# Background steps and weight halves ordered behind the sums and results, in the Strassen-like input projection of a one-core fp32 block

## The chip, the cores and the metric

The kernel runs on one core of one Trainium2 chip. The metric is the device time of one execution in microseconds (us). Engines are named as in the profile: PE is TensorE, DVE is VectorE, ACT is ScalarE, POOL is GpSimd, SP is SyncE. ACT, POOL and SP also issue DMAs.

## The reference

One layer of a hybrid encoder, sequence 1024, width 1024, float32:

```python
h = rmsnorm(x, g_pre_mix)
u_pool, q, k, v = split(h @ w_in)            # 512 columns each
y_pool = multiscale_pool(u_pool) @ w_br_pool # 4 groups of 128, windows 2, 4, 8, 16
y_sb   = stick_breaking_attention(q, k, v) @ w_br_sb     # 8 heads of 64
gates  = sigmoid(h @ w_gate + b_gate)        # 2 x 1024 columns
m = (gates[:, :1024] * y_pool + gates[:, 1024:] * y_sb) @ w_out
x = x + rmsnorm(m, g_post_mix)
h2 = rmsnorm(x, g_pre_mlp)
x = x + rmsnorm(relu(h2 @ w_up)**2 @ w_down, g_post_mlp)  # w_up to 4096 columns
```

## The kernel before, in words

Every large product of float32 matrices is made of three products on PE: an operand is cast into a high part on ACT (`hi`), and the rest is its low part, a subtraction on DVE (`lo`). Lines 110, 111 and 112 of the function `mm3` are hi·hi, hi(weight)·lo(data) and lo(weight)·hi(data). A weight tile `whi`/`wlo`, `a0hi`/`a0lo` and so on is thus usable in two steps: after its cast on ACT (line 1191) and after its subtraction on DVE (line 1192).

The kernel runs in stages: input norm, projection, attention with the pooling branch, output product, MLP. The change lies in the projection, `phase_project`. It computes the gates and q and k in twelve **pairs** (`PAIRS`: gates 0 to 4, q0, k0, q1, k1, gates 5 to 7). A pair is a 2x2 block product made with seven products instead of eight, in the Strassen manner. Each of the seven is twelve matmuls (four 128-row blocks times three) of 128x512 into one bank of PSUM, named `sw` in the profile. Their order is b11, b21, t2, t3, t1, t4, b22. The weight operands of a pair come from two loads of 512 KB (`r1`, `r2`, tiles `wraw` and `wrawx`): `a1` (all of r1, for b11 and b21), `a22` (half of r2, for t4), `sb` and `sa`, which are sums of halves and are made in place by four additions on DVE (lines 519 to 523), for t2/b22 and t3/t1. Tiles of `sb` are named `s0` or `s1`, of `a22` `a0` or `a1`, of `a1` and `sa` `w`.

The results of the seven products go through sums on DVE (lines 684 to 705): `c11`, `u`, `v`, `c22`, and from there to `result`: a gate goes through a sigmoid on ACT and a store from ACT's queue; q and k are split in a high part (ACT, line 542) and a low part (DVE, line 543) in a staging tile of `self.mx` (`m0` or `m1` in turns, so two are in flight) and stored by POOL to the scratch tensors `qscr`, from which SP loads the operands `qq` and `kk` of the attention. PSUM banks are taken in turns from three pools of 2, 2 and 3, so a bank is written again some seven products later, once DVE or ACT has read it.

Two kinds of work run beside the products. `sw_weights(i + 1)` is a generator that loads and splits the weights of the next pair; one step is taken after each product. `later` is a background generator, again a step or two after each product: for the four groups of the pooling branch it loads `u` (from `uscr`, ACT's queue), makes the window sums `win` (line 581, tiles `m1` and `m2`), splits them into `ph` and `pq`, multiplies them on PE (`dm`, and one `sw` bank), and stores `win` and `u` to `yscr` from POOL's queue; then for eight blocks it loads two shifted copies of v (`vpair`), subtracts them, splits the difference (`vs`) and stores it to `sscr`.

Which instruction stands where in an engine's queue is not the order of the source: a scheduler orders each engine's instructions by its own model of times, under the data dependencies. `tc.issue_after(ins)` adds an edge to that: what is written in its scope stands behind `ins` in the queue of `ins`'s own engine. It adds no wait between engines. `self.behind(ins)` is the same, or nothing where there is no `ins`. Each engine executes its queue strictly in order, so an instruction that waits holds everything behind it.

Of the kernel before, what the change touches and what calls it, by code (L numbers as in the profile page):

```python
# [32 lines left out]
P = 128  # L33
H = 512
# [18 lines left out]
class Block:  # L53
# [113 lines left out]
    def build(self):  # L167
# [55 lines left out]
        self.op7, self.sw, self.heads = {}, {}, {}  # L223
        self.phase_in()
# [303 lines left out]

    def staged(self, shape, dt, name):
        self.turn += 1  # L530
        return self.mx.tile(shape, dt, name=name, tag=f"m{self.turn % 2}")

    def result(self, kind, f, h, t, sign):

        nc = self.nc
        c = slice(h * H, h * H + H)
        if kind == "g":
            nc.scalar.activation(t, t, AF.Sigmoid, bias=self.vt[:, V_BG + f : V_BG + f + 1], scale=sign)
# [3 lines left out]
        nc.scalar.activation(e[:, 0, :], t, AF.Copy, scale=sc)  # L542
        nc.vector.scalar_tensor_tensor(
            out=e[:, 1, :], in0=t, scalar=sc, in1=e[:, 0, :].bitcast(F32), op0=ALU.mult, op1=ALU.subtract
        )
        for b in range(2):
            scr, s = self.qscr[kind == "k"][2 * f + b], e[64 * b : 64 * b + 64].bitcast(F32)
            nc.gpsimd.dma_start(scr[0:128, c].rearrange("(n p) c -> p n c", n=2), s)
            if kind == "q":
                nc.gpsimd.dma_start(scr[128:192, c], s[:, 0, :])  # L550

    def later(self, newbank):
# [19 lines left out]
        yield  # L572
        for g in range(4):
            iu = 3 * (g % 2)
            u = nxt_u
            cur, n = u, 0
            for i in range(g + 1):
                sh = 1 << i
                n = 1 + i % 2
                nxt = whole(n, name="win")  # L580
                nc.vector.tensor_add(nxt[:, sh:], cur[:, sh:], cur[:, : 1024 - sh])
                nc.vector.tensor_copy(nxt[:, :sh], cur[:, :sh])
                cur = nxt
                yield
# [9 lines left out]
            nc.scalar.copy(ph, cur)  # L594
            nc.vector.tensor_sub(pq, cur, ph.bitcast(F32))
# [17 lines left out]
        for t in range(NK):  # L613
# [9 lines left out]
            e = e.rearrange("p (h x) -> p h x", h=8)  # L623
            v = self.mx.tile([P, 8, P], F32R, name="vs", tag=f"m{n + 1}")
            nc.scalar.copy(v[:, :, 0:64], e)
# [20 lines left out]
    def phase_project(self):  # L646
# [16 lines left out]
        nxt = iter(())  # L663
# [12 lines left out]

        begun = {}

        def begin(i):
# [3 lines left out]
            nc.scalar.copy(u, product(w["a1"], 0, "b11"))  # L683
            nc.vector.tensor_add(c11, u, product(w["a1"], 512, "b21"))
# [3 lines left out]
        for i, (kind, f1) in enumerate(self.PAIRS):  # L688
            f2 = f1 + (8 if kind == "g" else 2)
            w = self.sw[i]  # L690
            nxt = self.sw_weights(i + 1) if i + 1 < len(self.PAIRS) else iter(())
# [3 lines left out]
            nc.vector.tensor_add(u, u, product(w["sb"], 0, "t2"))  # L695
            nc.vector.tensor_add(v, u, product(w["sa"], 0, "t3"))  # L696
            d = product(w["sa"], 512, "t1")
            nc.vector.tensor_add(c22, v, d)
            nc.vector.tensor_add(u, u, d)
# [3 lines left out]
            nc.vector.tensor_add(v, v, product(w["a22"], 0, "t4"))  # L703
            self.result(kind, f2, 0, v, -1.0)
            nc.vector.tensor_add(u, u, product(w["sb"], 512, "b22"))
            self.result(kind, f1, 1, u, 1.0)
        self.run(bg)
# [949 lines left out]
```

## Time and profile before

| | us |
|---|---|
| median of 3 runs | 1271.47 (1271.03 to 1273.86) |
| profiled execution, its own time | 1273.6 |
| its span in the profile | 1271.6 |
| PE busy in the span | 1242.0 (98%) |
| DVE busy | 968.9 (76%) |
| ACT busy | 622.6 (49%) |
| POOL busy | 179.7 (14%) |
| granted PE clock, mean | 0.997 |

The span is cut here at 98.5, 342, 365, 580, 760 and 1245 us. The projection's products lie between 98.76 and 347.4, the attention from there to about 580, the rest is the output product and the MLP. The profile's tables give, for a group of instructions, its busy time, the mean duration, and the idle time of the engine just before it with what ended that; rows of a timeline give the start, the duration and in brackets the idle time before with its releaser. A duration includes some overlap with the next instruction: DVE starts a 128x512 subtraction 0.60 us and a 128x1024 one 1.13 us after the one before, though the rows show 0.68 and 1.22.

### The profile page before, as it was taken

How to read it: one execution, taken by the hardware profiler on the slowest of the kernel's cores; microseconds unless marked ns; L12 is line 12 of the kernel's file. 1: busy time of each engine (PE TensorE's matmuls, PEld its weight loads, DVE VectorE, ACT ScalarE, POOL GpSimd, SP SyncE). 2: the span in 40 equal slices, each digit the busy share in tenths (PEclk: the TensorE clock that was granted, in tenths of full speed). 3: DMA queues.
4: the chain of work that ended last, by engine and by line, in shares of the span. 5: the costliest groups of instructions: out<-in, count | busy, mean ns of one | idle time of the engine just before them, and what ended most of it. 6: DMA issues, size and time to landing. Idle time of an engine off the chain costs nothing.

```text
span 1271.6 us, 16184 instructions
## 1 busy us (share of the span) xinstructions
PE 1242.0 (98%) x5707; PEld 1021.7 (80%) x5707; DVE 968.9 (76%) x1311; ACT 622.6 (49%) x994; POOL 179.7 (14%) x319
## 2 busy tenths in 40 slices
PE   9999999999999999999999999999999999999998
PEld 6887777887877877787778878888888888888887
DVE  8749687867578998877797879887865565776975
ACT  7237334333455565664556546455454443344452
POOL 1212111342101111101100002222121110001000
PEclk9999999999999999999999999999999999999999
DMA  6486878977899664456647677666549996556552
GB/s 218 152 245 161 241 195 232 315 262 251 300 356 332 218 209 103 130 129 220 214 139 259 199 247 257 236 225 226 180 181 336 305 302 227 198 198 248 193 197 67
DMA packets 110305, 283.00 MB, mean 223 GB/s; under 512 B 12464, under 2 KB 17584, under 8 KB 109072
## 3 DMA queue, kind: packets, MB, share of 16 engines
q1 hardware_dynamic: 65696, 165.28, 37.4%
q0 software_dynamic: 30992, 91.13, 25.2%
q10 hardware_dynamic: 13536, 25.57, 6.3%
q8 instruction: 45, 0.74, 0.2%
q14 instruction: 36, 0.29, 0.1%
HBM read 208.52 MB, written 94.37 MB: 238 GB/s over the span
## 4 chain that ended last, share of the span: by engine, by line
PE 73%; DMA 10%; DVE 8%; issue 5%; ACT 2%; POOL 1%; ACTq 0%; SPq 0%; DVEq 0%; POOLq 0%
PE d L110 17%; PE d L111 17%; PE d L112 17%; DMA vpair<-vscr 3%; PE dbr L112 3%; PE dbr L111 3%; PE o L838 3%; PE dbr L108 2%; DMA yscr<-win 2%; PE at L814 2%; DMA qscr<-qs 1%; DVE T L801 1%; PE z L794 1%; PE z L797 1%; DMA vscr<-ev 1%
## 5 line engine op out<-in xcount | busy, mean ns | idle before, releaser
L111 PE MATMUL d<-blo,whi 128*128 128x512 f32 (+1 forms) x456 | 172.3, 378 | 0.0
L112 PE MATMUL d<-bhi,wlo 128*128 128x512 f32 (+1 forms) x456 | 171.9, 378 | 0.0
L110 PE MATMUL d<-bhi,whi 128*128 128x512 f32 (+1 forms) x456 | 168.7, 378 | 0.0
L111 PEld LDWEIGHTS d<-blo,whi 128*128 128x128 f32 x456 | 85.7, 188 | 16.1
L112 PEld LDWEIGHTS d<-bhi,wlo 128*128 128x128 f32 x456 | 85.8, 188 | 16.0
L110 PEld LDWEIGHTS d<-bhi,whi 128*128 128x128 f32 x456 | 85.5, 188 | 15.8
L801 DVE TENSOR_TENSOR_SCAN T<-T,past 128x512 f32<-128x512 f32 (+3 forms) x64 | 84.8, 1345 | 8.5 <-ACT T L799 8.4
L111 PE MATMUL d<-b_lo,whi 128*128 128x512 f32 x196 | 76.2, 390 | 1.0 <-DVE b_lo L1083 1.0
L110 PE MATMUL d<-b_hi,whi 128*128 128x512 f32 x196 | 75.8, 390 | 0.1
L112 PE MATMUL d<-b_hi,wlo 128*128 128x512 f32 x196 | 74.2, 389 | 0.0
L78 DVE TENSOR_TENSOR wlo<-wraw,whi 128x1024 fp32r<-128x1024 f32 x45 | 54.8, 1219 | 16.1 <-ACT whi L76 14.4
L76 ACT CAST whi<-wraw 128x1024 fp32r<-128x1024 f32 x45 | 47.4, 1054 | 40.0 <-PE d L111 20.4
L799 ACT ACTIVATE T<-z 128x256 f32<-128x256 f32 (+2 forms) x96 | 44.5, 494 | 40.1 <-PE z L797 36.2
L1380 DVE TENSOR_TENSOR wlo<-slots_hi,whi 128x1024 fp32r<-128x1024 f32 x29 | 35.5, 1223 | 37.0 <-ACT whi L1378 36.9
L1378 ACT CAST whi<-slots_hi 128x1024 fp32r<-128x1024 f32 x29 | 30.5, 1052 | 67.1 <-PE d L111 60.9
L110 PE MATMUL sw<-h_hi,whi 128*128 128x512 f32 x144 | 56.6, 393 | 2.7 <-DVE v L696 0.8
L1378 ACT CAST whi<-slots_lo 128x1024 fp32r<-128x1024 f32 x27 | 28.4, 1053 | 62.3 <-PE d L111 52.1
L824 ACT CAST ahi<-at 128x512 fp32r<-128x512 f32 (+1 forms) x96 | 43.9, 483 | 28.2 <-PE at L814 23.7
L111 PE MATMUL sw<-h_lo,whi 128*128 128x512 f32 x144 | 56.1, 389 | 0.0
L825 DVE TENSOR_TENSOR alo<-at,ahi 128x512 fp32r<-128x512 f32 (+1 forms) x96 | 49.9, 543 | 7.6 <-ACT ahi L824 7.2
L112 PE MATMUL sw<-h_hi,wlo 128*128 128x512 f32 x144 | 55.5, 390 | 0.1
L1380 DVE TENSOR_TENSOR wlo<-slots_lo,whi 128x1024 fp32r<-128x1024 f32 x27 | 33.0, 1221 | 27.0 <-ACT whi L1378 26.9
(446 smaller groups left out, 3436.3 us busy)
## 6 DMA issues: line engine op xcount, KB each, us to landing
wraw<-w SPq DMA_DIRECT2D x57, 512.0 KB, 4.8
ext_b<-ascr SPq DMA_DIRECT2D x40, 512.0 KB, 7.1
wscr<-w POOLq DMA_DIRECT2D x32, 512.0 KB, 9.2
slots_hi<-w SPq DMA_DIRECT2D x10, 1024.0 KB, 8.1
slots_lo<-w SPq DMA_DIRECT2D x10, 1024.0 KB, 8.5
qq<-qscr SPq DMA_DIRECT2D x32, 256.0 KB, 5.7
pscr<-p SPq DMA_DIRECT2D x32, 256.0 KB, 3.9
u<-pscr ACTq DMA_DIRECT2D x32, 256.0 KB, 4.2
```

The source lines that it names most:

```text
L76: nc.scalar.copy(hi, raw)
L78: self.lows.append(nc.vector.tensor_sub(lo, raw, hi.bitcast(F32)).ins)
L110: nc.tensor.matmul(ps, wh, rh, start=first and i == 0, stop=False)
L111: nc.tensor.matmul(ps, wh, rl, start=False, stop=False)
L112: self.last_mm = nc.tensor.matmul(ps, wl, rh, start=False, stop=last and i == n - 1).ins
L799: self.after = nc.scalar.activation(f, z[:, :n], AF.Sigmoid, scale=-1.0)
L801: nc.vector.tensor_tensor_scan(f[:, ::-1], f[:, ::-1], past[:, ::-1], 1.0, ALU.mult, ALU.max)
L824: self.att_hi = nc.scalar.copy(hi[:, c:], at[:, c:]).ins
L825: self.att_lo = nc.vector.tensor_sub(lo[:, c:], at[:, c:], hi[:, c:].bitcast(F32)).ins
L838: t = nc.tensor.matmul(o[:, c0:], v, part[:, c0:], start=s == 0 and part is hi, stop=last and part is lo)
L1378: last_split[0] = nc.scalar.copy(hi, src).ins
L1380: last_split[1] = nc.vector.tensor_sub(lo, src, hi.bitcast(F32)).ins
```

## The change

It has five parts.

1. **Weights.** `sw_weights` (called once per pair, both loads at once, seven products ahead) is replaced in the loop by `sw_later`, a generator for pair j+2 that is started at product 7j+4 and does one small step per product: load of r1 ten products before the pair's first, load of r2 seven before it, then the casts and subtractions of `a1` and `a22`, the four sums, `sb`, and `sa`, a step each. Low parts come one product later than high parts.
2. **Order.** Each step of `sw_later` and of the background `later`, and each low part of q and k, is written in the scope of `behind(act_main)` and `behind(dve_main)`, where `act_main` and `dve_main` are the last cast or sigmoid of a result and the last sum of a product written so far. So on ACT and on DVE these stand behind them in the queue.
3. **Results of q and k.** A staging tile now holds the high parts of two results, and the low part is written over the result tile itself, one product later. Four results can be in flight where two could. The stores are 64x512 pieces: 80 DMAs from POOL's queue where there were 48, with the same bytes.
4. **Windows.** The tiles of the window sums go on alternating between `m1` and `m2` from one group to the next, where each group began at `m1`, so a group's first window is no longer written into the tile of which the group before is still being stored.
5. **Steps.** The background has some more steps (after the cast of `ph`, and around `vs`), one fewer for the first five blocks of v, and takes its double steps until product 42 where it was 36.

The numbers of instructions on PE, DVE and ACT are the same.

```diff
+    def sw_later(self, i):
...
+        pool = self.sw_pools[i % 2]
+        w = self.sw[i] = {}
+        r1 = load(a)
+        for _ in range(3):
+            yield
+        r2 = load(a + n)
+        a11, a12, a21, a22 = r1[:, :512], r1[:, 512:], r2[:, :512], r2[:, 512:]
+        yield
+        w["a1"] = high(r1, self.wp, "w", 3)
+        yield
+        low(w["a1"], r1)
+        yield
+        w["a22"] = high(a22, pool, f"a{i % 2}", 1, 512)
+        yield
+        low(w["a22"], a22)
+        nc.vector.tensor_add(a22, a21, a22)
+        nc.vector.tensor_add(a21, a11, a21)
+        nc.vector.tensor_add(a11, a11, a22)
+        nc.vector.tensor_add(a12, a12, a11)
+        yield
+        w["sb"] = high(r1, pool, f"s{i % 2}", 1)
+        yield
+        low(w["sb"], r1)
+        w["sa"] = high(r2, self.wp, "w", 3)
+        yield
+        low(w["sa"], r2)
...
-        e = self.staged([P, 2, H], F32R, f"{kind}s")
-        nc.scalar.activation(e[:, 0, :], t, AF.Copy, scale=sc)
-        nc.vector.scalar_tensor_tensor(
-            out=e[:, 1, :], in0=t, scalar=sc, in1=e[:, 0, :].bitcast(F32), op0=ALU.mult, op1=ALU.subtract
-        )
-        for b in range(2):
-            scr, s = self.qscr[kind == "k"][2 * f + b], e[64 * b : 64 * b + 64].bitcast(F32)
-            nc.gpsimd.dma_start(scr[0:128, c].rearrange("(n p) c -> p n c", n=2), s)
-            if kind == "q":
-                nc.gpsimd.dma_start(scr[128:192, c], s[:, 0, :])
+        if not self.stage:
+            e = self.staged([P, 2, H], F32R, f"{kind}s")
+            self.stage = [e[:, 0, :], e[:, 1, :]]
+        hi = self.stage.pop(0)
+        self.act_main = nc.scalar.activation(hi, t, AF.Copy, scale=sc).ins
+
+        def low():
+            nc.vector.scalar_tensor_tensor(
+                out=t.bitcast(F32R), in0=t, scalar=sc, in1=hi.bitcast(F32), op0=ALU.mult, op1=ALU.subtract
+            )
+            parts = (hi.bitcast(F32), t, hi.bitcast(F32)) if kind == "q" else (hi.bitcast(F32), t)
+            for b in range(2):
+                scr = self.qscr[kind == "k"][2 * f + b]
+                for n, e in enumerate(parts):
+                    nc.gpsimd.dma_start(scr[64 * n : 64 * n + 64, c], e[64 * b : 64 * b + 64])
+
+        self.lower.append(low)
...
+        n = 2
         for g in range(4):
             iu = 3 * (g % 2)
-            u = nxt_u
-            cur, n = u, 0
+            cur = u = nxt_u
             for i in range(g + 1):
                 sh = 1 << i
-                n = 1 + i % 2
+                n = 3 - n
...
         def product(w, at, name):
             d = newbank()
             self.half(d, w, at, name)
-            next(nxt, None)
-            next(bg, None)
             c = next(count)
-            if c % 6 == 5 and c < 36:
-                next(bg, None)
+            lower, self.lower = self.lower, []
+            with self.behind(self.act_main), self.behind(self.dve_main):
+                for f in lower:
+                    f()
+                if c % 7 == 4 and c // 7 + 2 < len(self.PAIRS):
+                    gens.append(self.sw_later(c // 7 + 2))
+                for gen in gens:
+                    next(gen, None)
+                for _ in range(2 if c % 6 == 5 and c < 42 else 1):
+                    next(bg, None)
             if c % 3 == 2 and c < 48:
                 self.sum_piece_with(self.last_mm)
             return d
+
+        def add(out, a, b):
+            self.dve_main = nc.vector.tensor_add(out, a, b).ins
```

The sums of the loop are made with `add` and keep their places. In the changed source their line is 750, the four weight sums are lines 570 to 573, the window sum is line 643, weight subtractions are lines 553 and 1268, the low part of q and k is line 603.

What the scheduler makes of it is shown at three places, before and after apart.

**DVE, pair 0 to pair 1.** `s0lo` is the last weight part of pair 0; `wraw_1045` is the second load of pair 1, and its addition with `wrawx` (line 521 before, 571 now) is what `sa` of pair 1, and so its products t3 and t1, wait for. Before, from the row behind `s0lo_995` on:

```order
L581 TENSOR_TENSOR win_1114<-u_1024 128x1023
L582 COPY win_1114<-u_1024 128x1
L684 TENSOR_TENSOR c11_1029<-u_1028,sw_1052 128x512
L1192 TENSOR_TENSOR a1lo_1066<-wraw_1045,a1hi_1065 128x512
L586 SCALAR_TENSOR_TENSOR win_1114<-win_1114,u_1024 128x1022
L589 TENSOR_TENSOR win_1114<-win_1114,rcnt_190 128x2
L519 TENSOR_TENSOR wraw_1045<-wraw_1045 128x512
L1192 TENSOR_TENSOR wlo_1048<-wrawx_1043,whi_1047 128x1024
L695 TENSOR_TENSOR u_1028<-u_1028,sw_1075 128x512
L590 TENSOR_TENSOR win_1114<-win_1114,u_1024 128x2
L521 TENSOR_TENSOR wraw_1045<-wrawx_1043,wraw_1045 128x512
```

The addition is the eleventh row behind `s0lo`, and one sum of a product (c11 of line 684) and one more (u of line 695) stand ahead of it. Now, from the twelfth row behind `s0lo_995` on:

```order
L750 TENSOR_TENSOR u_1030<-u_1030,sw_1109 128x512
L570 TENSOR_TENSOR wraw_1045<-wraw_1045 128x512
L652 TENSOR_TENSOR win_1105<-win_1105,u_1024 128x2
L750 TENSOR_TENSOR v_1067<-v_1067,sw_1136 128x512
L750 TENSOR_TENSOR u_1030<-u_1030,sw_1160 128x512
L571 TENSOR_TENSOR wraw_1045<-wrawx_1028,wraw_1045 128x512
L750 TENSOR_TENSOR c11_1181<-u_1180,sw_1213 128x512
L658 TENSOR_TENSOR pq_1153<-win_1105,ph_1152 128x1024
L572 TENSOR_TENSOR wrawx_1028<-wrawx_1028,wraw_1045 128x512
L553 TENSOR_TENSOR wlo_1175<-wraw_1045,whi_1174 128x1024
L573 TENSOR_TENSOR wrawx_1028<-wrawx_1028 128x512
L553 TENSOR_TENSOR wlo_1227<-wraw_1127,whi_1226 128x1024
```

The addition is the seventeenth row behind `s0lo`, and it stands behind all seven sums of pair 0 (the last is u with `sw_1160`, the product b22). `c11_1181`, which takes the product b21 of pair 1, stands behind it and ahead of `pq_1153`, of the third addition and of `wlo_1175`, the low part of `sa`.

**DVE, the start of pair 6** (the first k pair). `c11` is the sum that takes the pair's second product, b21; it can't run before PE has finished it. `wrawx_2027` and `wraw_1779` are the tiles in which `sb` is made (line 523 before, 573 now). Before:

```order
L705 TENSOR_TENSOR u_1841<-u_1841,sw_1990 128x512
L521 TENSOR_TENSOR wraw_2029<-wrawx_2027,wraw_2029 128x512
L626 TENSOR_TENSOR vs_1978<-vpair_1915,vs_1978 128x8x64
L522 TENSOR_TENSOR wrawx_2027<-wrawx_2027,wraw_2029 128x512
L523 TENSOR_TENSOR wrawx_2027<-wrawx_2027 128x512
L543 SCALAR_TENSOR_TENSOR qs_2005<-u_1841,qs_2005 128x512
L684 TENSOR_TENSOR c11_2013<-u_2012,sw_2036 128x512
L1192 TENSOR_TENSOR s1lo_2097<-wrawx_2027,s1hi_2096 128x1024
L1192 TENSOR_TENSOR wlo_2115<-wraw_2029,whi_2114 128x1024
```

All four weight sums, lines 519 to 523, stand ahead of `c11_2013`. Now:

```order
L571 TENSOR_TENSOR wraw_1855<-wraw_1779,wraw_1855 128x512
L603 SCALAR_TENSOR_TENSOR v_1881<-v_1881,qs_1975 128x512
L572 TENSOR_TENSOR wraw_1779<-wraw_1779,wraw_1855 128x512
L603 SCALAR_TENSOR_TENSOR u_1839<-u_1839,qs_1975 128x512
L685 TENSOR_TENSOR vpair_2001<-vpair_2001 128x512
L750 TENSOR_TENSOR c11_2008<-u_2007,sw_2033 128x512
L573 TENSOR_TENSOR wraw_1779<-wraw_1779 128x512
L553 TENSOR_TENSOR wlo_1999<-wraw_1855,whi_1998 128x1024
L553 TENSOR_TENSOR wlo_2047<-wrawx_1942,whi_2046 128x1024
L603 SCALAR_TENSOR_TENSOR c11_2008<-c11_2008,ks_2051 128x512
L553 TENSOR_TENSOR s0lo_1970<-wraw_1779,s0hi_1969 128x1024
```

The last weight sum (line 573), the low part `wlo_1999` of `sa`, and `s0lo_1970` of `sb` stand behind `c11_2008`. On PE the rows behind the last matmul of b21 were, before, those of t2 in a run, with `s0lo` in its third matmul:

```order
L112 MATMUL sw_2036<-h_hi0_777,wlo_1861 128x512
L110 MATMUL sw_2065<-ht2_hi_795,s0hi_1932 128x512
L111 MATMUL sw_2065<-ht2_lo_796,s0hi_1932 128x512
L112 MATMUL sw_2065<-ht2_hi_795,s0lo_1933 128x512
L110 MATMUL sw_2065<-ht2_hi_795,s0hi_1932 128x512
L111 MATMUL sw_2065<-ht2_lo_796,s0hi_1932 128x512
L112 MATMUL sw_2065<-ht2_hi_795,s0lo_1933 128x512
L110 MATMUL sw_2065<-ht2_hi_795,s0hi_1932 128x512
```

Now t3 (`sw_2078`), t1 (`sw_2097`), the next pair's b11 (`sw_2174`) and t2 (`sw_2055`) are each begun with the two matmuls that need no low part of the weight:

```order
L112 MATMUL sw_2033<-h_hi0_777,wlo_1876 128x512
L110 MATMUL sw_2078<-ht3_hi_797,whi_1998 128x512
L111 MATMUL sw_2078<-ht3_lo_798,whi_1998 128x512
L110 MATMUL sw_2097<-h_hi1_1002,whi_1998 128x512
L111 MATMUL sw_2097<-h_lo1_1003,whi_1998 128x512
L110 MATMUL sw_2174<-h_hi0_777,whi_2046 128x512
L111 MATMUL sw_2174<-h_lo0_778,whi_2046 128x512
L110 MATMUL sw_2055<-ht2_hi_795,s0hi_1969 128x512
L111 MATMUL sw_2055<-ht2_lo_796,s0hi_1969 128x512
L110 MATMUL sw_2123<-ht4_hi_799,a0hi_1918 128x512
```

The first matmul that needs `s0hi_1969`, which is cast from the tile that line 573 writes, is the seventh behind b21.

**PE, the end of the projection.** `z` is a score product of the first head of the attention, `kk` and `qq` its operands, loaded by SP; `kk` goes into the tile `m3`, from which `vs` of block 6 is stored to `sscr6`. Before, the first of them stood behind all products:

```order
L112 MATMUL sw_2876<-h_hi1_1002,s1lo_2724 128x512
L110 MATMUL sw_2876<-h_hi1_1002,s1hi_2723 128x512
L111 MATMUL sw_2876<-h_lo1_1003,s1hi_2723 128x512
L112 MATMUL sw_2876<-h_hi1_1002,s1lo_2724 128x512
L794 MATMUL z_2988<-kk_2897,qq_2896 128x512
L110 MATMUL dbr_2953<-yhi_2894,whi_2939 128x512
L111 MATMUL dbr_2953<-ylo_2895,whi_2939 128x512
L112 MATMUL dbr_2953<-yhi_2894,wlo_2940 128x512
```

Now two stand ahead of the last pair's t2, t4 and b22:

```order
L111 MATMUL sw_2867<-h_lo1_1003,whi_2793 128x512
L112 MATMUL sw_2867<-h_hi1_1002,wlo_2794 128x512
L870 MATMUL z_3012<-kk_2921,qq_2920 128x512
L873 MATMUL z_3012<-kk_2921,qq_2920 128x512
L110 MATMUL sw_2837<-ht2_hi_795,s1hi_2775 128x512
L111 MATMUL sw_2837<-ht2_lo_796,s1hi_2775 128x512
L110 MATMUL sw_2884<-ht4_hi_799,a1hi_2727 128x512
L111 MATMUL sw_2884<-ht4_lo_800,a1hi_2727 128x512
```

On POOL the store to `sscr6` stood ahead of the last twelve stores of q and k, and now stands behind all of them, last but one of the eight `sscr` stores.

More of the change, by code (lines that the diff above doesn't have):

```diff
@@ L223, in build @@
         self.op7, self.sw, self.heads = {}, {}, {}
+        self.stage, self.lower = [], []
         self.phase_in()
@@ L527, in sw_weights, with load, high, low @@
         w["sa"] = self.split_weights(r2, self.wp, "w", 3)
+    def sw_later(self, i):
+        nc = self.nc
+        kind, f = self.PAIRS[i]
+        a, n = (O_G + f, 8) if kind == "g" else (O_QK + 2 * f + (kind == "k"), 4)
+        def load(g):
+            if next(self.raws) < 2:
+                t = self.wp.tile([P, 1024], F32, name="wraw", tag="wraw", bufs=2)
+            else:
+                t = self.sw_pools[1].tile([P, 1024], F32, name="wrawx", tag="wrawx")
+            nc.sync.dma_start(t, self.w[g])
+            return t
+        def high(src, pool, tag, bufs, room=1024):
+            m = src.shape[-1]
+            hi, lo = (
+                pool.tile([P, room], F32R, name=f"{tag}{n}", tag=f"{tag}{n}", bufs=bufs)[:, :m] for n in ("hi", "lo")
+            )
+            nc.scalar.copy(hi, src)
+            return hi, lo
+        def low(pair, src):
+            nc.vector.tensor_sub(pair[1], src, pair[0].bitcast(F32))
+        pool = self.sw_pools[i % 2]
[24 more added lines that the diff above has]
+        low(w["sa"], r2)
     def staged(self, shape, dt, name):
@@ L662, in phase_project @@
         count = itertools.count()
-        nxt = iter(())
+        gens = [self.sw_later(1)]
+        for _ in range(3):
+            next(gens[0])
+        self.act_main = self.dve_main = None
         def product(w, at, name):
@@ L682, in begin @@
             u, c11 = part("u"), part("c11")
-            nc.scalar.copy(u, product(w["a1"], 0, "b11"))
-            nc.vector.tensor_add(c11, u, product(w["a1"], 512, "b21"))
+            self.act_main = nc.scalar.copy(u, product(w["a1"], 0, "b11")).ins
+            add(c11, u, product(w["a1"], 512, "b21"))
             self.result(kind, f, 0, c11, 1.0)
@@ L694, in phase_project @@
             u, v, c22 = begun[i], part("v"), part("c22")
[L695 to L696 removed]
+            add(u, u, product(w["sb"], 0, "t2"))
+            add(v, u, product(w["sa"], 0, "t3"))
             d = product(w["sa"], 512, "t1")
[L698 to L699 removed]
+            add(c22, v, d)
+            add(u, u, d)
             self.result(kind, f2, 1, c22, -1.0)
@@ L702, in phase_project @@
                 begin(i + 1)
-            nc.vector.tensor_add(v, v, product(w["a22"], 0, "t4"))
+            add(v, v, product(w["a22"], 0, "t4"))
             self.result(kind, f2, 0, v, -1.0)
-            nc.vector.tensor_add(u, u, product(w["sb"], 512, "b22"))
+            add(u, u, product(w["sb"], 512, "b22"))
             self.result(kind, f1, 1, u, 1.0)
+        for f in self.lower:
+            f()
         self.run(bg)
```

11 lines of the change are left out of this document (7 added, 4 removed).

## The prediction

> **What bounds the kernel now.** I read the page first. PE is busy almost throughout, so nothing but time that PE loses counts.
>
> ```profile
> PE 1242.0 (98%) x5707; PEld 1021.7 (80%) x5707; DVE 968.9 (76%) x1311; ACT 622.6 (49%) x994; POOL 179.7 (14%) x319
> ```
>
> Next the cut into stages; the columns are the stretch, its length, the busy time of PE, weight load, DVE, ACT and POOL, the granted clock, the DMA share and GB/s. The stretch of the change, and then the attention, where another 9.2 us of PE are idle that this change does not address:
>
> ```profile
> 98.50:342.00 243.50, 233.06 (x1011) 188.33 (x1010) 185.05 (x269) 102.19 (x141) 60.70 (x96) 1.00 0.80 242
> 365.00:580.00 215.00, 205.82 (x1082) 171.08 (x1081) 181.36 (x232) 130.18 (x292) 27.46 (x66) 0.99 0.64 197
> ```
>
> In the projection PE is idle 243.5 - 233.1 = 10.4 us at full clock; DVE has 58 us spare, ACT and POOL far more. Thirdly, who PE waits for there (total, times, longest):
>
> ```profile
> PE sw L110 <- DVE u L705: 2.8, 1, 2.8
> PE sw L110 <- ACT whi L1191: 2.6, 2, 1.5
> PE sw L110 <- DVE u L695: 1.8, 2, 1.3
> PE sw L110 <- DVE v L696: 0.8, 1, 0.8
> PE dm L111 <- DVE pq L595: 0.7, 1, 0.7
> PE sw L110 <- ACT vs L625: 0.7, 1, 0.7
> PE sw L110 <- DVE c L684: 0.7, 1, 0.7
> PE sw L112 <- DVE wlo L1192: 0.2, 1, 0.2
> ```
>
> The waits are ten, in all 10.3 us. Six stand for a sum that frees a bank (or a copy of v that holds such a sum up), three for a weight half, one for pooling. That is the whole prize. Checked by pace, the first, an undisturbed pair of rows 21 steps apart, and the last matmul of the stage:
>
> ```profile
> 98.76 0.39 PE L110 MATMUL sw<-h_hi,whi 128*128 128x512 f32 x1
> ...
> 294.68 0.39 PE L112 MATMUL sw<-ht_hi,wlo 128*128 128x512 f32 x1
> ...
> 299.44 0.39 PE L112 MATMUL sw<-h_hi,wlo 128*128 128x512 f32 x1
> ...
> 347.02 0.39 PE L112 MATMUL sw<-h_hi,s1lo 128*128 128x512 f32 x1
> ```
>
> (299.44 - 294.68)/21 = 0.227 us a matmul; 12 x 7 x 12 products and 24 for pooling are 1032, so 234 us would do where 248.3 were spent: 14 us lost, some of it before pair 1. Full success could save about 10 us.
>
> **Where the change bites: pairs 1 and 2.** PE reaches the product t3 of pairs 1 to 4 here (the first without a wait):
>
> ```profile
> 124.54 0.39 PE L110 MATMUL sw<-ht_hi,whi 128*128 128x512 f32 x1
> ...
> 148.33 0.50 PE L110 MATMUL sw<-ht_hi,whi 128*128 128x512 f32 x1 [1.49 <-ACT whi L1191]
> ...
> 172.76 0.50 PE L110 MATMUL sw<-ht_hi,whi 128*128 128x512 f32 x1 [1.09 <-ACT whi L1191]
> ...
> 193.43 0.47 PE L110 MATMUL sw<-ht_hi,whi 128*128 128x512 f32 x1 [1.28 <-DVE u L695]
> ```
>
> What DVE does ahead of them:
>
> ```profile
> 112.36 1.21 DVE L1192 TENSOR_TENSOR s0lo<-wraw,s0hi 128x1024 fp32r<-128x1024 f32 x1
> 113.50 1.21 DVE L581 TENSOR_TENSOR win<-u 128x1023 f32<-128x1023 f32 x1
> 114.63 0.14 DVE L582 COPY win<-u 128x1 f32<-128x1 f32 x1
> 114.70 0.67 DVE L684 TENSOR_TENSOR c<-u,sw 128x512 f32<-128x512 f32 x1
> 115.29 0.68 DVE L1192 TENSOR_TENSOR a1lo<-wraw,a1hi 128x512 fp32r<-128x512 f32 x1
> ...
> 119.51 0.68 DVE L521 TENSOR_TENSOR wraw<-wrawx,wraw 128x512 f32<-128x512 f32 x1
> ...
> 137.85 1.23 DVE L581 TENSOR_TENSOR win<-u 128x1023 f32<-128x1023 f32 x1 [7.01 <-DMA yscr<-win]
> ...
> 158.89 1.23 DVE L581 TENSOR_TENSOR win<-u 128x1023 f32<-128x1023 f32 x1 [3.97 <-DMA u<-uscr]
> ```
>
> From start to start a 512-wide operation takes 0.60, a 1024-wide one 1.13, a copy 0.07. ACT's side:
>
> ```profile
> 147.23 1.04 ACT L1191 CAST whi<-wrawx 128x1024 fp32r<-128x1024 f32 x1 [0.47 <-DVE wrawx L521]
> 148.18 1.05 ACT L1191 CAST whi<-wraw 128x1024 fp32r<-128x1024 f32 x1
> ...
> 150.34 0.36 ACTq L560 DMA_DIRECT2D u<-uscr  x1
> ```
>
> A weight cast is 1.0 us, and PE starts 0.1 us after it.
>
> *Pair 1.* The new queue has 17 rows from `s0lo` to the second addition. One low part of the weights `wm` falls behind `s0lo`, which so starts 0.6 us sooner, at 111.8. The rows and `s0lo` are four 1024-wide (4.5), eleven 512-wide (6.6), three tiny (0.2), so the addition ends at about 123.2, where it ended at 120.2. With the cast `whi` is there at 124.5, and PE stands at t3 by row count two matmuls later than before, at 125.0: in time. But the next row on DVE is `c11`, which takes b21 of pair 1, and PE ends that at 124.8; behind it stand `pq` (1.13), the third addition (0.6) and the low part of `sa` (1.13): 124.8 + 0.6 + 1.13 + 0.6 + 1.13 = 128.3. PE has ten matmuls to put in (2.3 us) and is there at 127.3. A new wait of 1.0 us (0 if `c11` is quicker, 2.5 with handoffs of 0.3 each and the sigmoids ahead of the cast).
>
> *Pair 2.* The wait of 7.0 us for the store of the old window goes (part 4). But it was not on PE's path, and in its place DVE now waits at the next sum u, whose product t2 of pair 1 ends on PE some 46 matmuls (10.5 us) behind the one that waited, so 139.0 with its result. Behind it, up to pair 2's second addition, stand fifteen rows: three 1024-wide, nine 512-wide, three tiny, 9.0 us: 148.1, and the cast makes 149.2; t3 starts at 149.4 against 148.33: +1.1. The ends: -1.5 if DVE's wait ends sooner (PE then arrives unhindered at 146.8), +2 with the wider handoffs of pair 1.
>
> *Pairs 3 and 4.* `u<-uscr` is still issued only when the pooling matmuls of the group before have been read, and its median and those of the other transfers on which something rests are (last number):
>
> ```profile
> u<-uscr ACTq DMA_DIRECT2D x4, 512.0 KB, 6.3
> qscr<-qs POOLq DMA_DIRECT2D x16, 256.0 KB, 5.0
> qscr<-qs POOLq DMA_DIRECT2D x16, 128.0 KB, 4.9
> sscr<-vs POOLq DMA_DIRECT2D x8, 512.0 KB, 6.9
> kk<-qscr SPq DMA_DIRECT2D x4, 256.0 KB, 6.3
> ```
>
> In the row at 158.89 it had taken 8.5 us from the issue at 150.34. In the new queue the first window stands ahead of every sum but one of its pair, so DVE waits there, and sums and weight sums with it. Issued at 156.5 (28 matmuls and a copy after 149.4) it lands at 162.8 to 165; then 14 rows of 8.4 us and a cast make t3 of pair 3 172.4 to 174.6, middle 173.5, against 172.76. The same walk for pair 4 (t2 ends at 184.8, u lands by 190.5, five operations and a cast) gives 194.4 against 193.43. So the loop of addition, cast, PE, sum runs a little behind, without gaining or losing much more: **+1.5 us by pair 5** in all (-1.5 to +4.5), with part 5's double steps inside it.
>
> **Pairs 5 to 11.** Here the background is short, and the waits removed are those of q and k. The largest:
>
> ```profile
> 300.01 0.63 ACT L542 ACTIVATE ks<-v 128x512 fp32r<-128x512 f32 x1 [3.35 <-DMA qscr<-ks]
> ...
> 300.68 0.69 DVE L543 SCALAR_TENSOR_TENSOR ks<-v,ks 128x512 fp32r<-128x512 f32 x1 [3.24 <-ACT ks L542]
> ...
> 302.62 0.50 PE L110 MATMUL sw<-ht_hi,a1hi 128*128 128x512 f32 x1 [2.79 <-DVE u L705]
> ```
>
> ACT waited for a store that still held the staging tile, DVE for ACT, the sum u stood behind, and PE wanted its bank. With four results in flight this goes: -2.9. The stretch's other two waits (`vs` and c, 0.7 each) are not of this kind and stay.
>
> Against it stands the order at pairs 6, 7 and 8, where the last sum for `sb`, or the low part of `sa`, is behind `c11`. From b21's last matmul: its result 0.39, handoff 0.1, c11 0.6, last addition 0.6, handoff 0.1, cast 1.0, handoff 0.1 = 2.9 us. PE has six matmuls to put in between, and would be at the one that needs it after 7 x 0.227 = 1.6: it waits 1.3 us. At pair 7 it is the low part of `sa`, behind `c11` and the third addition (0.39 + 0.1 + 0.6 + 0.6 + 1.13 + 0.1 = 2.9, again with six matmuls between), 1.3; at pair 8 as at pair 6. Together +3.9 (0 if the sum is done earlier than PE's order lets it, +5.2 with one more pair). Net of this stretch **+1.0** (-4.3, all waits gone, to +4).
>
> **The end.** Head 0's `kk` can be loaded only when `sscr6` has left its tile. Store and load are 6.9 + 6.3 and two issues of 0.6 and 0.3, 14.1 us, against the 68 matmuls (15.4 us) between the end of the product whose sum stands beside that `vs` and the first z. The medians just fit; one that is longer holds PE ahead of t2, which stands behind z. **+0.7** (0 to +3).
>
> **Stores.** 32 more from POOL, at the price of these rows:
>
> ```profile
> L548 POOL DMA_DIRECT2D qscr<-qs x16 | 9.6, 603 | 10.9 <-DVE qs L543 10.8
> L550 POOL DMA_DIRECT2D qscr<-qs x16 | 8.6, 542 | 13.0 <-ACT qs L542 13.0
> ```
>
> 32 x 0.54 to 0.60 = 17 to 19 us of POOL, which is idle for 243.5 - 60.7 = 183 us: hidden, and a piece lands in 4.9 us where a double one took 5.0. Taken as 0; without cover it is in the end's +3. [...]
>
> **The sum.** 1.5 + 1.0 + 0.7 = +3.2 us. The order of the attention also shifts where stages meet; no row prices that; I take 0, and a gain there has PE's idle 9.2 us of that stretch as its bound. The profiled execution's own time is 1273.6 (span 1271.6), so 1276.8 by its measure; it stands 2.1 above the median of the runs shown, and against that median of 1271.47 the forecast is **1274.7 us**.
>
> **Rivals.** *Faster.* Sums really come first: banks and sigmoids are freed as early as PE allows, and DVE's backlog, which I count as full from 112 to 124, drains in the 7 us that it waited. Then the waits of t3 in pairs 2 to 4 (1.5, 1.1, 1.3) go with that of u (2.9), 6.8 in all: 1264.7. For it speaks that six of the ten waits are for sums or what follows them; against it that t3's operand itself has been put behind the sums. It decides when `whi` of pair 2 is ready before 146.7. [...]
> *No change.* The loop of t3 settles within 1 us of the old one and pairs 6 to 8 cost what q and k save: 1271.5. For it: both terms are small differences of long chains.
> *Much slower.* Twelve stores of q and k and the later `sscr6` delay `kk` by twice its median, and z stands in front of 36 products: 1271.5 + 1.5 + 1.0 + 6.3 = 1280.3. It needs POOL late by more than 6 us at the end; its idle share speaks against it.
>
> **How the numbers follow.** About 0.2% (2.5 us) is what a measurement of this kernel can tell from no change. My case 0.44, of which 0.04 comes out within that bound; no change 0.23, of which 0.01 ends above it; faster 0.29; much slower 0.04. So faster 0.29, same 0.04 + 0.22 = 0.26, slower 0.40 + 0.01 + 0.04 = 0.45. The likeliest case alone has 1272 to 1279. The range reaches from the middle of the faster case, 1264.7, to 1280, and leaves out half of that case and the much slower one, 0.14 + 0.04.
>
> **What would show it.** In the profile after: PE idle in 98.5 to 345 of 12 to 15 us where it was 10.4; t3 of pair 2 at 149 to 150 behind ACT's cast; DVE's 7 us wait for `yscr` gone and one for PE's t2 in its place; three waits of 1 to 1.5 us for the `hi` of `sb` or the `lo` of `sa` at pairs 6 to 8; no wait of ACT for `qscr`. I am wrong if t3 of pair 2 starts before 147.5, or if the c11 waits are absent.

## The result, and the profile after

| | before | after |
|---|---|---|
| median of 4 runs, us | 1271.25 (1270.46 to 1273.86) | 1318.43 (1312.34 to 1321.60) |
| ratio, 95% interval | | 1.036 (1.0336 to 1.0384) |
| profiled execution, its own time; span | 1273.6; 1271.6 | 1312.3; 1310.6 |
| first to last `sw` matmul (projection) | 248.3 | 276.0 |
| from there to the first `d` matmul (attention) | 226.9 | 239.4 |
| from there to the end of the span | 697.6 | 697.7 |

The change costs 47 us by the medians and 39.0 by the profiled executions, of which after's is the fastest of its four. By the profiles 27.8 us are lost in the projection and 12.5 in the attention, 1.3 won ahead of them. One execution further below (of e13) took 4432.6 us, with PE busy for 4423.3 us over the 5707 matmuls that take 1257.8 in after; it is left out, of the table too.

The stage cut of after and of before at the same events. The columns are as in the prediction:

```profile
97.45:373.70 276.25, 250.05 (x1035) 199.53 (x1034) 184.99 (x270) 101.29 (x142) 72.89 (x126) 0.95 0.72 212
373.70:400.00 26.30, 20.88 (x96) 16.26 (x94) 12.67 (x21) 7.11 (x16) 1.50 (x4) 0.94 1.02 376
```

```profile
98.70:347.20 248.50, 238.06 (x1033) 192.47 (x1033) 187.42 (x272) 103.28 (x143) 60.70 (x96) 1.00 0.80 246
347.20:373.90 26.70, 25.66 (x137) 21.55 (x137) 18.98 (x30) 13.15 (x34) 1.91 (x6) 1.00 1.03 388
```

The same matmuls: PE is idle for 26.2 us where it was 10.4, and busy for 12 us more at a granted clock of 0.95. In the first 26 us of the attention it gets through 96 matmuls, not 137. Whom PE waits for in the projection of after:

```profile
PE sw L110 <- ACT whi L549: 13.5, 7, 4.2
PE sw L110 <- ACT s0hi L549: 7.4, 2, 6.9
PE dm L110 <- ACT ph L656: 2.6, 2, 1.4
PE sw L112 <- DVE wlo L553: 1.8, 1, 1.8
PE sw L110 <- DVE c L750: 0.4, 1, 0.4
```

The waits for sums and banks, six of ten before, are down to 0.4 us: in that the order does what it says. In their place stand the weights, 13.5 + 7.4 + 1.8 = 22.7 us. And DVE's waits, which tell why; first after, then before, for PE's products alone:

```profile
DVE u L750 <- PE sw L112: 62.4, 11, 8.5
```

```profile
DVE u L705 <- PE sw L112: 0.8, 1, 0.8
DVE u L695 <- PE sw L112: 0.4, 1, 0.4
```

DVE, which has time to spare, now stands 62 us in front of the sum u of t2, eleven times, once a pair, and behind it stand the sums of the next pair's weights. PE then waits for these. Work that ran beside PE now takes turns with it. Pair 8 shows the round, in rows of DVE, SP, ACT and PE in order of time:

```profile
280.06 1.23 DVE L553 TENSOR_TENSOR s1lo<-wrawx,s1hi 128x1024 fp32r<-128x1024 f32 x1 [0.52 <-ACT s1hi L549]
281.31 0.33 SPq L541 DMA_DIRECT2D wrawx<-w  x1
...
287.38 0.62 ACT L549 CAST a0hi<-wrawx 128x512 fp32r<-128x512 f32 x1 [6.82 <-DMA wrawx<-w]
...
289.03 0.69 DVE L750 TENSOR_TENSOR u<-u,sw 128x512 f32<-128x512 f32 x1 [7.14 <-PE sw L112]
...
295.15 0.68 DVE L571 TENSOR_TENSOR wrawx<-wraw,wrawx 128x512 f32<-128x512 f32 x1
...
296.31 1.04 ACT L549 CAST whi<-wrawx 128x1024 fp32r<-128x1024 f32 x1
...
297.41 0.50 PE L110 MATMUL sw<-ht_hi,whi 128*128 128x512 f32 x1 [1.62 <-ACT whi L549]
```

The load of pair 8 (SP) goes out 0.02 us after DVE has read the tile that it overwrites, so a late low part of one pair makes a late load of the next. In the projection ACT waits 62.0 us for weight loads, in before 27.0. DVE's wait for u is thus a mark of the lost time rather than its price: here it ended 1.0 us after the cast of `a0hi`, which had itself waited 6.8 us for the load, and most of the 10 us from that cast to t3 go to the ten rows from u to the sum of line 571 (6.1 us).

A measure of this is the lead: the time from the cast of a pair's `a22` (ACT, when its second load is there) to its first t3 on PE. For pairs 5 to 11 it was 17.7 to 23.3 us before (median 20.3), and is 8.6 to 17.9 after (median 9.9). At pair 8 before had, against the 10.0 us of the rows above:

```profile
251.40 0.62 ACT L1191 CAST a0hi<-wrawx 128x512 fp32r<-128x512 f32 x1 [0.83 <-DMA wrawx<-w]
...
273.79 0.39 PE L110 MATMUL sw<-ht_hi,whi 128*128 128x512 f32 x1
```

The period of t3 was 19.0 us, PE's own pace of 84 x 0.227, from pair 5 to pair 8; after it is 21 to 25 us up to pair 6 and 33 to the next.

### The profile page after: what moved, and what is told of

Same layout as the page of the kernel before. It is cut to its first block, busy times and chain, and to the rows that moved or that the text cites. A ratio compares the mean times of both kernels' runs of the same rounds, so it can differ in the third digit from the quotient of the medians.

```text
span 1310.6 us, 16170 instructions
## 1 busy us (share of the span) xinstructions
PE 1257.8 (96%) x5707; PEld 1029.2 (79%) x5707; DVE 968.1 (74%) x1311; ACT 621.7 (47%) x994; POOL 192.9 (15%) x351
## 4 chain that ended last, share of the span: by engine, by line
PE 67%; DMA 5%; DVE 5%; issue 3%; ACT 2%; POOL 0%; ACTq 0%; SPq 0%; DVEq 0%; POOLq 0%
PE d L112 16%; PE d L111 16%; PE d L110 16%; PE o L914 2%; PE dbr L111 2%; PE dbr L108 2%; PE dbr L112 2%; PE sw L110 2%; PE at L890 2%; PE sw L111 2%; PE sw L112 2%; DVE T L877 1%; DMA wraw<-w 1%; DMA gt<-gscr 1%; DMA ylo<-yscr 1%
## 5 line engine op out<-in xcount | busy, mean ns | idle before, releaser
L750 DVE TENSOR_TENSOR u<-u,sw 128x512 f32<-128x512 f32 x36 | 24.6, 683 | 62.4 <-PE sw L112 62.4
L78 DVE TENSOR_TENSOR wlo<-wraw,whi 128x1024 fp32r<-128x1024 f32 x45 | 54.9, 1220 | 18.1 <-ACT whi L76 16.6
```

Source lines behind the costliest of these rows:

```text
L78: self.lows.append(nc.vector.tensor_sub(lo, raw, hi.bitcast(F32)).ins)
```

## The experiments

Each edit is to the changed kernel unless it says otherwise. E is the pair of order edges of part 2 (`behind(act_main)`, `behind(dve_main)`).

| run | time, us | ratio to before | projection | attention |
|---|---|---|---|---|
| e1 no E | 1278.7 | 1.0063 (1.0039 to 1.0088) | 244.3 | 231.8 |
| e2 before, with E | 1285.9 | 1.0121 (1.0086 to 1.0156) | 255.2 | 234.0 |
| e3 old plan of weights, with E | 1275.1 | 1.0038 (1.0022 to 1.0054) | 248.9 | 232.5 |
| e4 before, parts 3 and 4 | 1271.4 | 1.0004 (0.9989 to 1.0019) | 248.2 | 227.3 |
| e5 new loads, old dates, with E | 1274.3 | 1.0044 (1.0029 to 1.0060) | 244.7 | 233.1 |
| e6 as e3, splits two products later | 1290.3 | 1.0168 (1.0149 to 1.0188) | 262.2 | 230.2 |
| e7 E on weights only | 1294.9 | 1.0189 (1.0161 to 1.0217) | 272.8 | 229.3 |
| e8 E on background and low parts only | 1280.4 | 1.0088 (1.0060 to 1.0115) | 250.5 | 231.6 |
| e9 faster background from product 64 | 1311.8 | 1.0302 (1.0272 to 1.0333) | 283.7 | 232.6 |
| e10 as e5, faster background | 1284.0 | 1.0099 (1.0081 to 1.0117) | 248.1 | 239.8 |
| e11 edge to DVE only | 1305.7 | 1.0289 (1.0256 to 1.0321) | 271.1 | 238.3 |
| e12 edge to ACT only | 1277.2 | 1.0046 (1.0030 to 1.0061) | 243.5 | 233.2 |
| e13 late gate stores from POOL | 1309.5 | 1.0316 (1.0288 to 1.0345) | | |
| e14 before, the same stores | 1273.0 | 1.0023 (1.0011 to 1.0036) | 248.8 | 230.0 |
| e15 as e5, the same stores | 1275.2 | 1.0039 (1.0026 to 1.0053) | 245.1 | 231.8 |
| e16 e13 again | 1314.1 | 1.0355 (1.0322 to 1.0389) | 279.5 | 237.0 |

**e1**, the edges left out:

```diff
-            with self.behind(self.act_main), self.behind(self.dve_main):
+            with contextlib.nullcontext():
```

> The changed kernel with the order edges of part 2 left out (the steps and low parts are written in no scope); all else as changed. Theory O (the order behind sums and results eats the lead of the weights): the lead from the cast of a22 to t3 grows from 9 to 10 us to over 14 at most pairs and the time falls to 1268 to 1285. Theory P (the new plan of one small weight step per product, and low parts a product later, is what is late): stays above 1305. Theory S (split stores and staging): stays above 1305 too, with waits at POOL and qscr.

1278.7 us. As theory O has it: the lead in pairs 5 to 11 is 18.4 to 30.8 us, DVE waits 2.9 us for the sums u, and the projection is 4 us shorter than before's. So without the edges the new plan of weights, with parts 3 to 5 beside it, does no harm to the projection in this profile.

**e2**, only the edges, on the kernel before:

```diff
-            next(nxt, None)
-            next(bg, None)
...
+            with self.behind(self.act_main), self.behind(self.dve_main):
+                next(nxt, None)
+            with self.behind(self.act_main), self.behind(self.dve_main):
+                for _ in range(2 if c % 6 == 5 and c < 36 else 1):
+                    next(bg, None)
```

> The kernel before with only the order edges of part 2 around its weight and background steps (old plan of weights, old staging and windows). Theory O: slower than 1290, with DVE waiting for PE's products ahead of weight sums. Theory P or S: within 1% of before, 1265 to 1283.

1285.9: slower, as O says, but short of its 1290 and of after's 1318, and DVE's waits for u are 2.9 us only. The edges alone cost 15 us here, by the profiles 7 in the projection, with other waits (PE for `wlo` 6.0 us, for `ph` 4.9), and 7 in the attention.

**e3**, the changed kernel with the old `sw_weights`:

```diff
-                if c % 7 == 4 and c // 7 + 2 < len(self.PAIRS):
-                    gens.append(self.sw_later(c // 7 + 2))
-                for gen in gens:
-                    next(gen, None)
+                next(nxt, None)
...
+            nxt = self.sw_weights(i + 1) if i + 1 < len(self.PAIRS) else iter(())
```

> The changed kernel with the old plan of weights: both loads at the pair's start seven products ahead, a split per step, but still behind the sums and results. Theory O: still above 1295. Theory P: back to 1270 to 1285.

1275.1, what theory P said. With e1 this leaves neither alone: without edges the new plan costs 8 us, with the old plan the edges cost 5, both together 47. (With the old plan and the edges, but without parts 3 to 5, e2 lost 15; which of these parts makes the difference stays open.)

**e4**, parts 3 and 4 on the kernel before (staging and windows as in the change's diff, no edges, old weights):

> The kernel before with only parts 3 and 4: four results of q and k in flight with low parts a product later and 64x512 stores, and the windows alternating through the groups. Theory S: above 1290. Theories O and P: 1262 to 1275, since the wait of 2.8 us for the sum u behind ks goes and DVE's wait of 7.0 us for yscr goes.

1271.4, the same as before. Theory S is out. The gains that O and P allowed did not come either.

From e1 to e4 came theory D: an edge makes the date of a step in the plan its earliest date. Without edges, the scheduler takes a step as soon as its data are there. For pair j+1 the old plan has the four sums at products 7j+1 and 7j+2 and `sa` at 7j+4; the new has them at 7j+4 and 7j+6 to 7. Those two to three products are the lead.

**e5**, the new loads, but the steps at the old dates:

```diff
-        yield
         w["a1"] = high(r1, self.wp, "w", 3)
-        yield
         low(w["a1"], r1)
         yield
         w["a22"] = high(a22, pool, f"a{i % 2}", 1, 512)
-        yield
         low(w["a22"], a22)
         nc.vector.tensor_add(a22, a21, a22)
+        yield
         nc.vector.tensor_add(a21, a11, a21)
...
         w["sb"] = high(r1, pool, f"s{i % 2}", 1)
+        low(w["sb"], r1)
         yield
-        low(w["sb"], r1)
         w["sa"] = high(r2, self.wp, "w", 3)
-        yield
         low(w["sa"], r2)
```

> The changed kernel with the weight steps at the old dates: the loads stay where the change put them (r1 ten, r2 seven products ahead), the casts, sums and low parts are done as the old plan had them, the last (sa) at the fifth product of the pair before instead of the seventh and eighth; all order edges kept. Theory D (the edges turn the dates of the plan into earliest dates, and the new dates are two to three products too late): 1268 to 1285, with the cast of a22 15 us or more ahead of t3. Rival B (what hurts is the background behind the sums, with its waits for DMAs ahead of weight sums): stays above 1300.

1274.3 us: with every edge kept, all but 3 of the 47 us are gone by the medians, all but 5 to 6 by the ratio. The lead is 20.2 to 25.3 us, ACT waits 13.6 us for weight loads, and DVE's wait for u:

```profile
DVE u L747 <- PE sw L112: 3.5, 2, 2.9
```

**e6**, the opposite, e3 with all splits from the second pair on two products later:

```diff
+        if i:
+            for _ in range(2):
+                yield
         w["a1"] = self.split_weights(r1, self.wp, "w", 3)
```

> The run with the old plan of weights behind the sums (1275 us) with every split two products later, the loads unmoved: about the dates of the change. Theory D: 1290 or more. Rival B: within 1% of 1275, since the background's edges are the same. Rival L (the loads' dates or the single steps of the new generator matter, not the splits): within 1% of 1275.

1290.3, 15 us more than e3, 0.3 over theory D's bound and 2.6 over that of its rivals, and DVE's waits for u, 45.0 us in the projection, are back:

```profile
DVE u L748 <- PE sw L112: 45.0, 12, 7.0
```

**e7 and e8**, the edges on one kind of step:

```diff
-            with self.behind(self.act_main), self.behind(self.dve_main):
+            with contextlib.nullcontext():
                 for f in lower:
                     f()
+            with self.behind(self.act_main), self.behind(self.dve_main):
...
+            with contextlib.nullcontext():
                 for _ in range(2 if c % 6 == 5 and c < 42 else 1):
                     next(bg, None)
```

This is e7; in e8 the steps of the weights stand in no scope and the other two keep it.

> The changed kernel with the order edges on the weight steps alone; background and low parts of q and k in no scope. Theory D: above 1295. Rival B: below 1285.

> The changed kernel with the order edges on the background and the low parts alone; the weight steps in no scope. Theory D: 1265 to 1285. Rival B: above 1300, with DVE's waits for vpair ahead of c11 or of a weight sum as in the changed kernel.

1294.9 and 1280.4. e7's projection (272.8) has all but 3 us of the loss, its DVE waits 39.0 us for u and its lead is 8.1 to 17.0. e8 is e1 within 2 us in total, with 6 us more in its profiled projection. So the weights' edges are most of what costs in the projection. The background's edges cost more where those stand: 24 us by the medians, 14 by the profiled executions, of which 10 are in the attention. e7 lies 0.1 us under theory D's bound.

**e11 and e12**, one edge of the two (this is e11, e12 keeps `self.act_main`):

```diff
-            with self.behind(self.act_main), self.behind(self.dve_main):
+            with self.behind(self.dve_main):
```

> The changed kernel with the edges to DVE's last sum kept and those to ACT's last cast or sigmoid left out. Theory D, as the traces of the changed kernel show it (weight sums queued on DVE behind sums that wait for PE): still above 1300. Rival A (the casts behind ACT's sigmoids are what is late): below 1290.

> The changed kernel with the edges to ACT's last cast or sigmoid kept and those to DVE's last sum left out. Theory D: below 1292. Rival A: above 1300.

DVE's waits for u, e11's and e12's:

```profile
DVE u L750 <- PE sw L112: 61.3, 11, 8.2
```

```profile
DVE u L750 <- PE sw L112: 9.9, 5, 4.4
```

1305.7 and 1277.2: it is the queue of DVE. e11 has after's projection within 5 us, with a median lead of 10.3; e12's is 243.5.

**The attention.** At the projection's end, SP and POOL in before and after stand so to the last `sw` matmul: the last store to `sscr` at -23.0 before, -9.4 after; the loads of `kk` of the first two heads at -55.8 and -7.1 before, -13.4 and +1.6 after; the third load of `yhi` at -6.7 and +1.9. **e9** and **e10** bring the background forward, in the changed kernel and in e5:

```diff
-                for _ in range(2 if c % 6 == 5 and c < 42 else 1):
+                for _ in range(2 if c % 6 == 5 and c < 42 or c >= 64 else 1):
```

> The changed kernel with two background steps instead of one after every product from number 64 on, so that the last blocks of v, and with them kk and the pooling results for the attention, come sooner; nothing else. Theory T (the 12.5 us that the changed kernel loses between its last product and the output product come from the late end of the background): that stretch falls from 239 to 232 us or less and the time to 1305 to 1313. Theory G (they come from the late last pair itself and from its results): the stretch stays at 237 or more, the time above 1314. The projection stays at 274 to 278 us in both.

> The run with the weight steps at the old dates (1274.3 us, projection 244.7, attention 233.1) with the same faster background from product 64 on. Theory T: the attention falls to 227 to 230 and the time to 1266 to 1271, at or just under before. Theory G: unchanged, 1272 to 1276.

e9: the last `sscr` at -21.2, `kk` at -25.6 and -12.9, and the attention 232.6, 6.8 less than after: theory T, but for 0.6 us. Its projection was 283.7, though, out of what both allowed, and it is 7 us behind after's at pair 5 already. The edit is not the cause: up to 344 us PE, DVE, ACT and POOL execute the same rows in the same order as in after. Of the 7.7 us 1.9 are longer waits of PE, and 5.4 are slow matmuls, 71 of them at half pace where after has 39 (more on these below). e10 missed by 13 us: the loads came sooner here too (second `kk` at -3.1 for +2.0) and the attention became longer. Its row:

```profile
PE z L867 <- ACT T L872: 6.7, 2, 6.0
```

ACT stood in front of a gate store. In after it is the same in ACT's queue, where the sigmoid of the last u ends at 381.15 and the next wide T (the exponentials of the attention) waits:

```profile
380.43 0.72 ACT L591 ACTIVATE u<-u,vt 128x512 f32<-128x512 f32 x1
384.92 0.33 ACTq L594 DMA_DIRECT2D gscr<-v  x1
387.64 0.33 ACTq L594 DMA_DIRECT2D gscr<-u  x1
388.02 0.98 ACT L875 ACTIVATE T<-z 128x512 f32<-128x512 f32 x2 [6.87 <-DMA ylo<-yscr]
```

**e13 to e16** take the gate stores of the last two pairs off ACT's queue, in the changed kernel, in before and in e5:

```diff
-            return nc.scalar.dma_start(self.gscr[f][:, c], t)
+            return (nc.gpsimd if f % 8 >= 6 else nc.scalar).dma_start(self.gscr[f][:, c], t)
```

> The changed kernel with the gate stores of the last two pairs issued from POOL's queue instead of ACT's; order edges and all else kept. Theory Q (where the attention begins, ACT stands in front of the issue of the last gate stores while SP's loads keep the DMA engines full, and the first exponentials T queue behind: 6.9 us in the changed kernel): the stretch from the last product to the output product falls from 239 to 233 us or less, the time to 1306 to 1313. Theory T (late kk, y and v loads alone): the stretch stays at 237 or more.

> The kernel before with the gate stores of the last two pairs issued from POOL's queue. Theory Q: ACT's 3.2 us in front of its first T go; 1266 to 1270. Theory T: unchanged, 1270 to 1273.

> The run with the weight steps at the old dates (1274.3 us; its projection was shorter than before's, its attention longer) with the gate stores of the last two pairs from POOL's queue. No wait of ACT for such a store shows in that run's attention, so theory Q gives no gain there: 1272 to 1276. If the time falls below 1270 it is the later loads that the stores delayed.

> The run with the gate stores of the last two pairs on POOL's queue again, since its profiled execution was one in which every matmul took several times as long, and so showed nothing of the stretch. Theory Q: the stretch from the last product to the output product 233 us or less, no wait of ACT for ylo or gt ahead of T. Theory T: 237 or more.

e16's profile shows no wait of ACT for a transfer ahead of T, and the attention is 237.0, 2.4 us shorter. PE now waits there for the loads themselves:

```profile
PE z L870 <- DMA kk<-qscr: 3.2, 1, 3.2
...
PE dbr L111 <- DMA ylo<-yscr: 2.1, 1, 2.1
```

So theory Q is out for most of after's loss there; its stores may be 2 us of it, by one profiled execution each. Theory T has e9 and e16 for it and e10 against it, and in e1 the first two loads of `kk` go out at -17.1 and -12.2 and the attention is still 5 us longer than before's: the late loads are a part of the loss, and the rest stays open. The total can't tell: e13 and e16, one kernel, have 1.0316 and 1.0355, on either side of what the edit could win. e14, 1273.0, is where theory T had it and 0.2% slower where theory Q had it faster; e15 is unchanged, as forecast. No run beat the kernel before.

## Why the prediction was wrong

*The start, right up to pair 3.* t3 of pairs 1 to 4 was forecast at 125.0, 149.4, 173.5 and 194.4:

```profile
126.18 0.50 PE L110 MATMUL sw<-ht_hi,whi 128*128 128x512 f32 x1 [1.44 <-ACT whi L549]
...
149.68 0.79 PE L110 MATMUL sw<-ht_hi,whi 128*128 128x512 f32 x1 [3.25 <-ACT whi L549]
...
174.80 0.50 PE L110 MATMUL sw<-ht_hi,whi 128*128 128x512 f32 x1 [1.42 <-ACT whi L549]
...
198.12 0.39 PE L110 MATMUL sw<-ht_hi,whi 128*128 128x512 f32 x1
```

Off by 0.3 to 1.3 us, and 3.7 at pair 4. DVE's wait for `yscr` fell from 8.5 to 1.9 us and its wait for t2 came instead, at 139.4 where 139.0 was forecast. From the t3 of pair 0 to that of pair 5 after takes 118.25 us and before 112.47, 5.8 more; but t2 has changed sides with t3 in the new order, so PE puts in 444 matmuls there instead of 456. For the same work the loss is 5.8 + 12 x 0.227 = 8.5 us, against the forecast +1.5 (to +4.5).

*"So the loop ... runs a little behind, without gaining or losing much more": the step that failed.* It was right that addition, cast, t3, t2 and sum u had become one chain of PE's length and over. But I took it for a matter of the four pooling groups and counted pairs 5 to 11 by single waits, +1.0. In before the lead grows there to 20 us, since nothing dates the splits. With the edges it doesn't grow: the chain, which leads over the freed tile and its load too, goes on, 21 to 33 us a pair from pair 5 to pair 9 against 19 to 20. From t3 of pair 5 to that of pair 11 after takes 138.2 us and before 119.7, with 504 matmuls in both: **+18.5** where +1.0 was forecast. 13.6 of them lie between pairs 6 and 7, where without lead two waits of DVE for loads reached PE (below). e5 shows that it is the dates behind the edges, e11 that it is DVE's queue.

*The c11 waits: the place right at pair 6, the size wrong.* 1.3 us at pairs 6, 7 and 8 were forecast. 7.0 came at pair 6, at the matmul foreseen. At pair 7 4.2 came, but at t3 and for the sum of line 571, which stands ahead of c11; at pair 8 1.6 at t3, and 0.4 + 0.4 at c11 and behind it. Pair 6, on DVE, then ACT, then PE:

```profile
239.16 0.82 ACTq L680 DMA_DIRECT2D vpair<-vscr  x2
...
247.78 0.69 DVE L685 TENSOR_TENSOR vpair<-vpair 128x512 f32<-128x512 f32 x1 [5.11 <-DMA vpair<-vscr]
248.38 0.68 DVE L750 TENSOR_TENSOR c<-u,sw 128x512 f32<-128x512 f32 x1
248.98 0.68 DVE L573 TENSOR_TENSOR wraw<-wraw 128x512 f32<-128x512 f32 x1
```

```profile
249.15 0.63 ACT L600 ACTIVATE ks<-c 128x512 fp32r<-128x512 f32 x1 [6.08 <-DMA qscr<-qs]
249.70 1.04 ACT L549 CAST s0hi<-wraw 128x1024 fp32r<-128x1024 f32 x1
```

```profile
250.80 0.79 PE L110 MATMUL sw<-ht_hi,s0hi 128*128 128x512 f32 x1 [6.95 <-ACT s0hi L549]
251.39 0.63 PE L111 MATMUL sw<-ht_lo,s0hi 128*128 128x512 f32 x1
251.81 0.63 PE L110 MATMUL sw<-ht_hi,a0hi 128*128 128x512 f32 x1
252.24 0.63 PE L111 MATMUL sw<-ht_lo,a0hi 128*128 128x512 f32 x1
```

In the row order that I showed, the subtraction of `vpair` stood directly above `c11`, and I priced it at its 0.6 us, not at its load: 8.6 us from the issue, 5.1 of them DVE's wait. At pair 7 DVE waited 4.1 us for the next such load, ahead of the sum of line 571. Before had such waits too (17.2 us in all), and little behind them that was due (0.7 us of PE's waits).

*"No wait of ACT for `qscr`": nearly.* ACT's waits for `qscr` fell from 18.1 us in six to the one of 6.1 us in the rows above, and that one is not the staging tile's price: its row also needs the sum c11, which ended at 249.06, within 0.1 us of ACT's start, behind the load of `vpair`. But e4 shows that the gain of 2.9 us which I counted for part 3 comes to nothing in the total even without edges.

*Not in the sum: the clock.* After the wait of 7 us the matmuls stand 0.427 us apart, not 0.227, for eight rows, and the granted clock from 251 to 256 us is 0.64. In the projection of after 39 steps from start to start lie at 0.42 to 0.43, 7.8 us over the pace; all steps over 0.3 without a wait in them are 12.8 us over it, on top of the waits. In before these are 2.1 us, with one step at 0.44. The difference of 10.7 is most of the 12 us by which PE is busier. The waits of 3.3, 7.0 and 4.2 us were followed by nine, seven and six steps at 0.42 to 0.43; but two groups of shorter waits (1.4 and 1.2; 1.6, 0.4 and 0.4 us) had five and eleven, and the wait of 2.8 us in before had none, so the length of a single wait doesn't decide it here. What does is not shown.

*The end.* +0.7 was forecast, for z in front of t2 waiting for `kk`. That wait did not come: PE has none from t3 of pair 11 to the last product. The 14.1 us there, for 10.7 in before, are 62 matmuls where there were 48, since t2 stands behind t3 now. The loss of 12.5 us came behind the projection, in the attention, which I took as 0: 8.0 us more of idle PE, and 4.5 more of busy PE. The second `kk` and half of the `y` loads, which in before were issued ahead of the last product, now go out behind it with those of `v`, where the DMA engines are full in both kernels (1.02 and 1.03). As said above, this explains a part.

*The stores.* POOL's busy time in the stage rose from 60.7 to 72.9 us, hidden, and e4, which has all the pieces, is at 1.0004: the 32 stores more don't show in the time, as forecast.

The ratio of e1 has a part that stays open: its median is 5 us above its profiled execution (1273.4), and no trace shows why.

## What to carry to other kernels

An order edge turns a plan's date from a wish into an earliest date. Before adding one, count for every step behind it the lead that it has now, over the whole stage, and what stands between the edge's instruction and the reader: if the edge's instruction itself waits for the engine that reads the step, two engines that worked side by side take turns, and the tile that the step frees for the next load comes late too (here DVE stood 62.4 us in front of u, and ACT waited 62.0 us for weight loads). Price a row that is put ahead of something due at its operand's arrival, not at its own duration (at pair 6 a wait of 5.1 us ahead of 0.69). Once PE's waits get long, look for slow matmuls behind them: here six to nine at half pace (0.43 us a step for 0.23), 1.2 to 1.8 us, followed each wait of 3.3 to 7.0 us. And before two stretches are compared from one product to another, count the matmuls in them.

## What the runs showed of the hardware that was not expected

ACT's gate stores stand in its queue among its exponentials. In after the last two were issued 3.8 and 2.4 us behind the row before them (384.92 and 387.64), and the exponentials waited with them, 6.87 us, which the profile puts down to `ylo`. The trace has, right ahead of each of the two issues, a wait of ACT on a semaphore (118, then 110) with which the store then goes out, and the transfer that had gone out with it last was a `ylo` load of SP. These loads took 8.7 and 10.0 us, landed at 384.84 and 387.57, and the stores followed within 0.1 us. In before a gate store likewise went out at 343.60, when a `qq` load with the store's semaphore (116) had landed at 343.52. So these three stores waited for transfers that have nothing to do with their data; why they had a semaphore in common the record does not show.

One order of rows did not give one time. After, e16 and e9 have the same rows in the same order on PE, DVE, ACT and POOL up to 344 us, and their projections take 276.0, 279.5 and 283.7 us, with 39, 55 and 71 steps at half pace (granted clock of the whole execution 0.985, 0.982 and 0.980). The slow steps (all over 0.3 us without a wait) make 2.8 of the 3.5 us and 5.4 of the 7.7 us between them, the waits of PE 0.6 and 1.9.
